# Attention's second head turned one place later, the query norms behind a weighing, and four sums of a down projection behind the next weights

## The chip, the cores and the metric

The kernel runs on one core of a Trainium2 chip. TensorE multiplies (PE in the profile; PEld is its weight load), VectorE and ScalarE (DVE, ACT) do the elementwise work, GpSimd (POOL) and SyncE (SP) mainly start transfers. The metric is the device time of one execution in microseconds (us); lower is better. Times are medians over runs.

## The reference

Two decoder layers over 512 tokens of width 1024, all in float32. Layer 0 is a Mamba-2 mixer with a convolutional feed-forward; then keys and values are made once; layer 1 is differential attention with eight heads, again with a feed-forward. What the change touches, cut to it:

```python
q = rms_norm((rms_norm(x, ln_g) @ q_w).reshape(b, s, 8, 2, 64), q_norm_g)   # query norms
logits = einsum(q, k) * 64 ** -0.5 + bias          # two maps per head, causal
p = softmax(logits)
attn = p[:, :, 0] - lam * p[:, :, 1]               # the "weighing"
o = rms_norm(einsum(attn, v), subln_g) * (1 - lam_init)   # a head's output
x = x + o @ out_w
u = causal_dwconv(rms_norm(x, ln_g) @ up_w)        # feed-forward of layer 1
x = x + (silu(u_gate) * u_up) @ down_w             # the "down" product
```

## The kernel before

Every float32 product is made of three products of rounded halves: a weight is split into `wh` (rounded, by ACT) and `wl` (the rest, by DVE: weight minus `wh`), and TensorE adds `wh*xh`, `wh*xl` and `wl*xh` in one PSUM bank (L207 to L209, L1325 to L1327, L1133 to L1136). `chunk(key)` takes the next weights of a fixed plan and starts the split of those two places ahead. There are eight PSUM banks: four for large products ("mm") and four for everything else ("aux": logits, transposes, values and some of the down products).

**Attention.** In this part the order on TensorE is written out by hand (`manual_schedule`); the orders of DVE and ACT are made by a list scheduler from the same program. A head is three units (`Unit`), named head_part: `lg3_0` is head 3, part 0. A unit goes through `logits` (TensorE into `lg` banks, DVE adds the bias and takes the maxima `mx`, ACT takes the exponentials with their sums `sm`), `weigh` (DVE: reciprocal `rc`, factor, then one sum per block of rows at L1525; part 0 has two of them, 128 and 256 wide), `turn` (TensorE transposes the weighed map into an `at` bank, L1534, ACT copies it out, L1535) and `values` (TensorE into `po`, L1545, ACT into `ot`). When a head's three units have their values, `normed_out` scales its output `ot` (ACT square, DVE sum `so`, two ACT steps, three small DVE steps and `ot` times `so` at L1558), and `turned_out` transposes it (`oT`, L1564) and splits it into `oh` (ACT) and `ol` (DVE) for the output product. `ots.append([t + 5, u])` sets at which place of the written order `turned_out` is issued.

Between the units TensorE works on what `fill` gives: the value projection `v0`, the queries of heads 4 to 7 (`q1`), the values `v1`, and the first output product. Each `next(fill)` is two blocks of 128 tokens against one chunk of weights (12 matmuls). The queries `q1` come out as four tiles `knq1_0` to `knq1_3`; `head_norm` multiplies them by their norms on DVE (L1350) and registers in `late` two transposes (`ktq1`, L1357) that TensorE does inside `v1`, and that ACT copies into `qT1`, which the logits of head 4 read.

**Down product of layer 1.** The feed-forward's 22 pairs of columns are done in three parts (0 to 5, 6 to 13, 14 to 21). After each part, `down_tokens` makes the down product with seven products instead of eight (keys 1, 2, 5, 7, 6, 3, 4, in this order). After product 6, DVE combines for b = 0 and 1: the running sum `run_sum` takes product 6, is subtracted from one stretch of the residual `xr`, takes product 7, and goes into two more stretches of `xr` (L1139). Product 3 is then added, product 4 last. `wl_s14_0_0` and `wl_s14_0_2` are the low halves of product 4's weights in the first part; `wl_g1_6` is that of the first gate weights of the next part. Here the scheduler orders all engines.

Of the kernel before, what the change touches and what calls it, by code (L numbers as in the profile page):

```python
# [18 lines left out]
P = 128  # L19
# [22 lines left out]
def trunk_kernel(ctx: ExitStack, tc, x, ssm_ln_g, ssm_in_w, ssm_conv_w, ssm_conv_b, ssm_dt_bias,  # L42
# [950 lines left out]
    def ffn(l, norm, bp, gnext, nnext):  # L993
        with tc.tile_pool(name="ffn_h%d" % l, bufs=1) as hp, tc.tile_pool(name="ffn%d" % l, bufs=1) as fp:
# [65 lines left out]
            def combine(key, m, p0, c, nq):  # L1060

                n = nq * ncol
                if m == "2" or (m == "4" and not l):
                    t = wrp.tile([P, 1024], F32, tag="raw", name="wr_" + key)
                    sync.dma_start(view(t, nq), source(p0, c, nq, 1, 0 if l or m == "2" else 1))
                elif l:
                    t = raws["x" if m == "7" else "y" if m == "3" else "z"][c // 2]
                    if m == "7":
                        dve.tensor_tensor(out=t[:, :n], in0=t[:, :n], in1=raws["y"][c // 2][:, :n], op=ALU.add)
                else:  # L1070
                    t = raws["x" if m in "17" else "z"][c]
                wh = wp.tile([P, 1024], F32R, tag="wh", name="wh_" + key)
                wl = wp.tile([P, 1024], F32R, tag="wl", name="wl_" + key)
                act.activation(wh[:, :n], t[:, :n], AF.Copy)
                dve.tensor_tensor(out=wl[:, :n], in0=t[:, :n], in1=wh[:, :n].bitcast(F32), op=ALU.subtract)  # L1075
                ready.append((key, view(wh, nq), view(wl, nq)))
                more = ({"1": (0, 1), "5": (1, 1), "6": (1, 0)} if l else {"1": (0, 1), "5": (0, 0), "6": (1, 0)}).get(m)
                if more:
                    plus(t, p0, c, nq, *more)
# [41 lines left out]
            def down_tokens(p0, n, sides, last):  # L1121

                nq = n // 2
                side = {"1": 0, "2": 1, "4": 2, "5": 3, "6": 4, "7": 5, "3": 6}

                def products(m, bs, qs, pss, first=True, end=True, cols=slice(0, 512)):

                    for low in range(2):
                        for b in bs:
                            for q in qs:  # L1130
                                h, w = (t[:, side[m], b * P:(b + 1) * P] for t in sides[q][:2])
                                if low:
                                    pe.matmul(pss[b], h, ws[q][1][:, cols], start=False, stop=end and q == qs[-1])  # L1133
                                    continue
                                pe.matmul(pss[b], h, ws[q][0][:, cols], start=first and q == qs[0], stop=False)  # L1135
                                pe.matmul(pss[b], w, ws[q][0][:, cols], start=False, stop=False)  # L1136

                def add(t, v, op=ALU.add):
                    dve.tensor_tensor(out=t, in0=t, in1=v, op=op)  # L1139

                def to(b, c, n=512):
                    return xr[:, b, c:c + n]

                def store(b, c, eng):
                    eng.dma_start(out[0, b * P:(b + 1) * P, c:c + 256], to(b, c, 256))

                def stores(bs, c):
                    for b in bs:
                        for j in range(2):
                            store(b, c + 256 * j, sync if j else act)  # L1150

                for m in SEVEN[1]:
                    pss = [(aux_bank if m in "273" else mm_bank)("ps_s%s_%d_%d" % (m, p0, b)) for b in range(2)]
                    cut = last and m == "4"
                    ws = {}
                    for q0 in range(0, nq, 2):
                        wh, wl = chunk("s1%s_%d_%d" % (m, p0, q0))
                        qs = range(q0, min(nq, q0 + 2))
                        for q in qs:
                            ws[q] = wh[:, q - q0, :], wl[:, q - q0, :]  # L1160
                        if not cut:
                            products(m, range(2), qs, pss, q0 == 0, qs[-1] == nq - 1)
                    if cut:
                        products(m, (0,), range(nq), pss)
                    for b in range(2):
                        r = run_sum[:, b, :]
                        if m == "1":
                            add(to(b, 0), pss[b])
                            act.activation(r, pss[b], AF.Copy)
                        elif m == "2":  # L1170
                            add(to(b, 0), pss[b])
                        elif m == "5":
                            add(to(b, 512), pss[b])
                            add(to(2 + b, 512), pss[b])
                        elif m == "7":
                            seven = pss
                        elif m == "6":
                            add(r, pss[b])
                            add(to(b, 512), r, ALU.subtract)
                            add(r, seven[b])  # L1180
                            add(to(2 + b, 512), r, ALU.subtract)
                            add(to(2 + b, 0), r)
                        elif m == "3":
                            add(to(b, 512), pss[b])
                        elif not (cut and b):
                            add(to(2 + b, 0), pss[b])
                    if last and m in "263":
                        stores((2, 3) if m == "6" else (0, 1), 0 if m == "2" else 512)
                    if cut:
                        stores((2,), 0)  # L1190
                        products(m, (1,), range(nq - 1), pss)
                        add(to(3, 0), pss[1])
                        for j in range(2):
                            end = aux_bank("end%d" % j)[:, :256]
                            products(m, (1,), [nq - 1], {1: end}, cols=slice(256 * j, 256 * (j + 1)))
                            add(to(3, 256 * j, 256), end)
                            store(3, 256 * j, act if j else sync)
# [85 lines left out]
    with tc.tile_pool(name="att", bufs=1) as ap, ExitStack() as later:  # L1283
# [61 lines left out]

        def head_norm(key, kn, ss, dst, gcol, where):
            rsqrt_act(ss, ap, key, [P, NT, 8], 64)
            for b in range(NT):
                v = kn[b].rearrange("p (a q) -> p a q", a=8)
                dve.tensor_tensor(out=v, in0=v, in1=ss[:, b, :].unsqueeze(2).to_broadcast([P, 8, 64]),  # L1350
                                  op=ALU.mult)

            def turned(bs):
                for b in bs:
# [263 lines left out]
        with tc.manual_schedule(engines={mybir.EngineType.PE}):  # L1618
# [17 lines left out]
            def values(t):  # L1636
                u = us[t]
                u.values()
                if u.part == len(PARTS) - 1:
                    valued_heads.append(u)  # L1640
                    ots.append([t + 5, u])

            def norm_heads():
                while valued_heads:
# [108 lines left out]
```

## Time and profile before

| | |
|---|---|
| median of 3 runs | 1323.74 us (1322.02 to 1325.03) |
| the profiled execution | 1323.59 us, of which the profile's span is 1321.9 us |
| TensorE busy | 1313.3 us, 99% of the span |
| VectorE busy | 1094.1 us, 83% |
| ScalarE busy | 722.5 us, 55% |
| mean granted TensorE clock | 0.999 |

The profile is of one execution. Its views have one row for a group of instructions: the engine, the source line, the operation, the tiles it writes and reads, how often it ran, and in brackets how long the engine had sat idle before it and what released it. In the timeline, the first number is the start from the beginning of the span, the second how long it took; neighbours of one kind are merged (x4). TensorE's instructions overlap: one begins before the last has drained, so its rate is read from the distances of the starts. Buffer numbers are left out in the timeline: `lg`, `at`, `oT`, `so` there are those of whichever head stands at that time.

### The profile page before, as it was taken

The page shows a single profiled execution, that of the slowest core. Times are in us where ns is not written, and L with a number is a line of the kernel's source. Part 1 is how long each engine was busy: PE and PEld are TensorE (multiplying, and loading weights), DVE is VectorE, ACT ScalarE, POOL GpSimd, SP SyncE. Part 2 cuts the span into 40 slices and gives each one's busy share as a digit, 9 for nine tenths or more (in the row PEclk, how much of TensorE's full clock was granted, in tenths as well). Part 3 has the DMA queues.
Part 4 walks back from the last instruction along what each step waited for, and adds up shares of the span by engine and source line. Part 5 has one row for each costly group of instructions (what it writes and reads, how often), then busy time and mean ns, then how long its engine had stood idle before and what let it go on. Part 6 is the DMA issues. An engine that isn't in the chain of part 4 may idle for free. (4 is left out here: it accounts for less than half of the span.)

```text
span 1321.9 us, 18303 instructions
## 1 busy us (share of the span) xinstructions
PE 1313.3 (99%) x6771; PEld 1097.8 (83%) x6771; DVE 1094.1 (83%) x1834; ACT 722.5 (55%) x1176; POOL 176.2 (13%) x243
## 2 busy tenths in 40 slices
PE   9999999999999999999999999999999999999998
PEld 8878888888888988898889887767888878888887
DVE  7989888788878878886889877778778978887887
ACT  6696554743454545543556676767654534444452
POOL 4330200300121401110113210000020100010001
PEclk9999999999999999999999999999999999999999
DMA  7553533532235657674856854211225445453635
GB/s 209 161 154 87 146 108 103 145 92 79 80 96 149 118 149 205 167 155 128 225 143 143 208 129 125 64 57 56 65 80 159 97 119 178 106 99 112 191 64 128
DMA packets 202553, 167.85 MB, mean 127 GB/s; under 512 B 7580, under 2 KB 175904, under 8 KB 202464
## 3 DMA queue, kind: packets, MB, share of 16 engines
q1 hardware_dynamic: 176080, 124.93, 31.8%
q0 software_dynamic: 22928, 36.46, 14.8%
q10 hardware_dynamic: 3456, 5.30, 1.1%
q8 instruction: 53, 0.87, 0.3%
q14 instruction: 36, 0.29, 0.1%
HBM read 160.21 MB, written 6.44 MB: 126 GB/s over the span
## 5 line engine op out<-in xcount | busy, mean ns | idle before, releaser
L207 PE MATMUL ps_u<-xgh,wh_u 128*128 128x512 f32 x352 | 137.4, 390 | 0.0
L209 PE MATMUL ps_g<-xgh,wl_g 128*128 128x512 f32 x352 | 137.1, 389 | 0.0
L207 PE MATMUL ps_g<-xgh,wh_g 128*128 128x512 f32 x352 | 137.1, 389 | 0.0
L209 PE MATMUL ps_u<-xgh,wl_u 128*128 128x512 f32 x352 | 137.0, 389 | 0.0
L208 PE MATMUL ps_g<-xgl,wh_g 128*128 128x512 f32 x352 | 137.0, 389 | 0.0
L208 PE MATMUL ps_u<-xgl,wh_u 128*128 128x512 f32 x352 | 136.9, 389 | 0.0
L207 PE MATMUL ps_in<-xgh,wh_in 128*128 128x512 f32 x304 | 122.9, 404 | 0.0
L209 PE MATMUL ps_in<-xgh,wl_in 128*128 128x512 f32 x304 | 119.7, 394 | 0.0
L208 PE MATMUL ps_in<-xgl,wh_in 128*128 128x512 f32 x304 | 119.1, 392 | 0.0
L209 PEld LDWEIGHTS ps_g<-xgh,wl_g 128*128 128x128 f32 x352 | 66.1, 188 | 14.0 <-DVE wl_g L158 0.3
L208 PEld LDWEIGHTS ps_g<-xgl,wh_g 128*128 128x128 f32 x352 | 66.1, 188 | 13.7
L1228 PE MATMUL ps_s<-sl,wh_s 128*128 128x256 f32 x308 | 77.5, 283 | 0.0
L209 PEld LDWEIGHTS ps_u<-xgh,wl_u 128*128 128x128 f32 x352 | 66.1, 188 | 13.7
L1227 PE MATMUL ps_s<-sh,wh_s 128*128 128x256 f32 x308 | 77.5, 283 | 0.0
L208 PEld LDWEIGHTS ps_u<-xgl,wh_u 128*128 128x128 f32 x352 | 66.1, 188 | 13.6
L207 PEld LDWEIGHTS ps_g<-xgh,wh_g 128*128 128x128 f32 x352 | 66.1, 188 | 13.6
L207 PEld LDWEIGHTS ps_u<-xgh,wh_u 128*128 128x128 f32 x352 | 66.1, 188 | 13.5
L1118 ACT ACTIVATE sh<-vg 128x256 fp32r<-128x256 f32 (+1 forms) x44 | 23.0, 524 | 96.0 <-DVE vg L1266 96.0
L1047 POOL DMA_DIRECT2D wz<-in_ffn_down_w_dram x36 | 44.2, 1295 | 233.3 <-DVE wl_s L1075 156.1
L1262 ACT ACTIVATE vg<-vg 128x512 f32<-128x512 f32 x44 | 27.8, 633 | 78.7 <-DVE vg L1019 78.7
L1019 DVE SCALAR_TENSOR_TENSOR vg<-ug,cf,vg 128x511 f32<-128x511 f32 x88 | 65.8, 748 | 5.5 <-ACT vg L1017 4.1
L147 ACT ACTIVATE wh_u<-wr_u 128x1024 fp32r<-128x1024 f32 x44 | 46.6, 1059 | 42.5 <-PE ps_g L208 35.4
(430 smaller groups left out, 3527.1 us busy)
## 6 DMA issues: line engine op xcount, KB each, us to landing
wr_g<-in_ffn_up_w_dram SPq DMA_DIRECT2D x44, 512.0 KB, 3.9
wr_u<-in_ffn_up_w_dram SPq DMA_DIRECT2D x44, 512.0 KB, 4.0
wr_in<-in_ssm_in_w_dram SPq DMA_DIRECT2D x40, 512.0 KB, 3.9
wz<-in_ffn_down_w_dram POOLq DMA_DIRECT2D x27, 512.0 KB, 5.9
m<-cumd POOLq DMA_DIRECT2D x16, 512.0 KB, 5.0
wr_out<-in_ssm_out_w_dram SPq DMA_DIRECT2D x16, 512.0 KB, 3.5
wr_s<-in_ffn_down_w_dram SPq DMA_DIRECT2D x13, 512.0 KB, 3.8
xT<-in_ffn_down_w_dram SPq DMA_DIRECT2D x10, 512.0 KB, 7.0
```

Of the source, the lines that this page charges most:

```text
L147: return act.activation(self.wh[:, :self.n], self.raw[:, :self.n], AF.Copy)
L207: pe.matmul(ps, wh, xh, start=start, stop=False)
L208: pe.matmul(ps, wh, xl, start=False, stop=False)
L209: return pe.matmul(ps, wl, xh, start=False, stop=stop).ins
L1019: dve.scalar_tensor_tensor(out=v[:, s:], in0=u[:, :T - s], scalar=col(2 - s), in1=v[:, s:], op0=ALU.mult, op1=ALU.add)
L1047: pool.dma_start(view(t, nq), source(p0, c, nq, j, i), accum_op=ALU.add)
L1118: act.activation(sh[:, o], v, AF.Copy)
L1227: pe.matmul(v[:, b], wh[:, q, cols], h, start=q == 0, stop=False)
L1228: pe.matmul(v[:, b], wh[:, q, cols], w, start=False, stop=False)
L1262: act.activation(ga, ga, AF.Silu)
```

## The change

Three edits. The output of head 1 is turned at `t + 6` instead of `t + 5`. The four multiplications of the `q1` norms are no longer issued when the queries are done, but registered in `late`, behind block 3 of the first `v1` chunk. In the first part of layer 1's down product (`p0 == 0`), the four sums of `run_sum` into the lower two blocks of `xr` are issued with product 3, behind the last low half that `combine` has made by then (`state["low"]`).

```diff
--- before.py
+++ after.py
@@ -1072,7 +1072,8 @@
                 wh = wp.tile([P, 1024], F32R, tag="wh", name="wh_" + key)
                 wl = wp.tile([P, 1024], F32R, tag="wl", name="wl_" + key)
                 act.activation(wh[:, :n], t[:, :n], AF.Copy)
-                dve.tensor_tensor(out=wl[:, :n], in0=t[:, :n], in1=wh[:, :n].bitcast(F32), op=ALU.subtract)
+                state["low"] = dve.tensor_tensor(out=wl[:, :n], in0=t[:, :n], in1=wh[:, :n].bitcast(F32),
+                                                 op=ALU.subtract).ins
                 ready.append((key, view(wh, nq), view(wl, nq)))
                 more = ({"1": (0, 1), "5": (1, 1), "6": (1, 0)} if l else {"1": (0, 1), "5": (0, 0), "6": (1, 0)}).get(m)
                 if more:
@@ -1143,6 +1144,11 @@
 
                 def store(b, c, eng):
                     eng.dma_start(out[0, b * P:(b + 1) * P, c:c + 256], to(b, c, 256))
+
+                def second_half(b):
+                    r = run_sum[:, b, :]
+                    add(to(2 + b, 512), r, ALU.subtract)
+                    add(to(2 + b, 0), r)
 
                 def stores(bs, c):
                     for b in bs:
@@ -1178,9 +1184,12 @@
                             add(r, pss[b])
                             add(to(b, 512), r, ALU.subtract)
                             add(r, seven[b])
-                            add(to(2 + b, 512), r, ALU.subtract)
-                            add(to(2 + b, 0), r)
+                            if p0:
+                                second_half(b)
                         elif m == "3":
+                            if not p0:
+                                with tc.issue_after(state["low"]):
+                                    second_half(b)
                             add(to(b, 512), pss[b])
                         elif not (cut and b):
                             add(to(2 + b, 0), pss[b])
@@ -1345,10 +1354,16 @@
 
         def head_norm(key, kn, ss, dst, gcol, where):
             rsqrt_act(ss, ap, key, [P, NT, 8], 64)
-            for b in range(NT):
-                v = kn[b].rearrange("p (a q) -> p a q", a=8)
-                dve.tensor_tensor(out=v, in0=v, in1=ss[:, b, :].unsqueeze(2).to_broadcast([P, 8, 64]),
-                                  op=ALU.mult)
+            def normed():
+                for b in range(NT):
+                    v = kn[b].rearrange("p (a q) -> p a q", a=8)
+                    dve.tensor_tensor(out=v, in0=v, in1=ss[:, b, :].unsqueeze(2).to_broadcast([P, 8, 64]),
+                                      op=ALU.mult)
+
+            if key == "q1":
+                late.append(((0, 3), normed))
+            else:
+                normed()
 
             def turned(bs):
                 for b in bs:
@@ -1638,7 +1653,7 @@
                 u.values()
                 if u.part == len(PARTS) - 1:
                     valued_heads.append(u)
-                    ots.append([t + 5, u])
+                    ots.append([t + (6 if u.h == 1 else 5), u])
 
             def norm_heads():
                 while valued_heads:
```

Line numbers in the changed kernel are up to 15 higher. What the edits do to the engines' orders stands in three places.

**Place 1: attention, around the turn of head 1's output.** TensorE, before: `po2_1` are the values of head 2's second unit, `oT1` the transposes of head 1's output, `ps_v1_2` a value product with the chunk `v1_0`.

```order
L1545 MATMUL po2_1_8281<-vt0_6961,at2_1_8180 128x128
L1545 MATMUL po2_1_8281<-vt1_6962,at2_1_8180 128x128
L1545 MATMUL po2_1_8281<-vt2_6963,at2_1_8180 128x128
L1564 MATMUL oT1_8286<-ident_77,ot1_8028 128x128 x4
L1325 MATMUL ps_v1_2_8234<-wh_v1_0_7964,xgh_86 128x512
L1326 MATMUL ps_v1_2_8234<-wl_v1_0_7965,xgh_86 128x512
L1327 MATMUL ps_v1_2_8234<-wh_v1_0_7964,xgl_87 128x512
```

TensorE in the changed kernel, where `oT1` now stands (one chunk later, `v1_2`, behind the transposes of the queries):

```order
L1336 MATMUL ps_v1_1_8229<-wh_v1_2_8088,xgl_87 128x512
L1372 MATMUL ktq1_2_8359<-ident_77,knq1_2_8157 128x128 x4
L1372 MATMUL ktq1_3_8365<-ident_77,knq1_3_8162 128x128 x4
L1579 MATMUL oT1_8371<-ident_77,ot1_8028 128x128 x4
L1334 MATMUL ps_v1_2_8230<-wh_v1_2_8088,xgh_86 128x512
L1335 MATMUL ps_v1_2_8230<-wl_v1_2_8089,xgh_86 128x512
L1336 MATMUL ps_v1_2_8230<-wh_v1_2_8088,xgl_87 128x512
```

The four transposes moved behind 24 matmuls of `v1`, one whole unit's turn, logits and values (`at3_0`, `lg3_2`, `po2_2`) and the four `ktq1` transposes.

VectorE at the same time, before: the first weighing of `lg3_0` (128 wide), the query norms, the second weighing (256 wide), the low half of head 1's output.

```order
L1525 SCALAR_TENSOR_TENSOR lg3_0_0_8192<-lg3_0_1_8193,sm3_0_8191,lg3_0_0_8192 128x128
L1350 TENSOR_TENSOR knq1_0_8106<-knq1_0_8106,ssq1_7751 128x512
L1350 TENSOR_TENSOR knq1_1_8111<-knq1_1_8111,ssq1_7751 128x512
L1350 TENSOR_TENSOR knq1_2_8157<-knq1_2_8157,ssq1_7751 128x512
L1350 TENSOR_TENSOR knq1_3_8162<-knq1_3_8162,ssq1_7751 128x512
L1525 SCALAR_TENSOR_TENSOR lg3_0_0_8192<-lg3_0_1_8193,sm3_0_8191,lg3_0_0_8192 128x256
L1568 SCALAR_TENSOR_TENSOR ol1_8292<-oT1_8286,c2_89,oh1_8291 128x512
```

VectorE in the changed kernel:

```order
L1540 SCALAR_TENSOR_TENSOR lg3_0_0_8192<-lg3_0_1_8193,sm3_0_8191,lg3_0_0_8192 128x128
L1540 SCALAR_TENSOR_TENSOR lg3_0_0_8192<-lg3_0_1_8193,sm3_0_8191,lg3_0_0_8192 128x256
L1360 TENSOR_TENSOR knq1_0_8106<-knq1_0_8106,ssq1_7751 128x512
L1360 TENSOR_TENSOR knq1_1_8111<-knq1_1_8111,ssq1_7751 128x512
L1360 TENSOR_TENSOR knq1_2_8157<-knq1_2_8157,ssq1_7751 128x512
L1360 TENSOR_TENSOR knq1_3_8162<-knq1_3_8162,ssq1_7751 128x512
L1519 ISA lg3_2_0_8306,mx3_2_8304<-lg3_2_0_8308,tb3_8186 128x512
```

The second weighing moved ahead of the four norms, and `ol1` went some rows further down, behind the weighing of `lg3_2`.

**Place 2: attention, some microseconds later.** ScalarE, before, from the exponentials of `lg3_2` on: the copies of the turned queries into `qT1`, the two steps of head 2's output norm `so2`, the high half of the first output weights.

```order
L1512 ACTIVATE lg3_2_1_8316,sm3_2_8314<-lg3_2_1_8316,mx3_2_8313 128x512
L1358 ACTIVATE qT1_6960<-ktq1_0_8350,c2_89 128x4x128
L1358 ACTIVATE qT1_6960<-ktq1_1_8356,c2_89 128x4x128
L495 ACTIVATE so2_8381<-rsm_o2_8384 128x4
L496 ACTIVATE so2_8381<-so2_8381 128x4
L1358 ACTIVATE qT1_6960<-ktq1_2_8368,c2_89 128x4x128
L1358 ACTIVATE qT1_6960<-ktq1_3_8374,c2_89 128x4x128
L147 ACTIVATE wh_ao0_0_8447<-wr_ao0_0_8445 128x1024
```

ScalarE in the changed kernel:

```order
L1527 ACTIVATE lg3_2_1_8307,sm3_2_8305<-lg3_2_1_8307,mx3_2_8304 128x512
L1373 ACTIVATE qT1_6960<-ktq1_0_8341,c2_89 128x4x128
L1373 ACTIVATE qT1_6960<-ktq1_1_8347,c2_89 128x4x128
L1373 ACTIVATE qT1_6960<-ktq1_2_8359,c2_89 128x4x128
L1373 ACTIVATE qT1_6960<-ktq1_3_8365,c2_89 128x4x128
L1582 ACTIVATE oh1_8376<-oT1_8371,c2_89 128x512
L495 ACTIVATE so2_8381<-rsm_o2_8384 128x4
L496 ACTIVATE so2_8381<-so2_8381 128x4
L147 ACTIVATE wh_ao0_0_8447<-wr_ao0_0_8445 128x1024
```

`oh1`, the high half of head 1's output, now stands behind all four copies, and the two steps of `so2` behind `oh1`. On VectorE the sum that makes `so2` stands behind `ol1`, which reads `oh1`.

**Place 3: the down product of layer 1's first part.** VectorE, before: `run_sum` takes product 7, goes into `xr` four times, then come the low halves of product 4, the sums of product 3, and the next part's gate weights.

```order
L1139 TENSOR_TENSOR run_sum1_9342<-run_sum1_9342,ps_s7_0_0_10026 128x512
L1139 TENSOR_TENSOR run_sum1_9342<-run_sum1_9342,ps_s7_0_1_10027 128x512
L1139 TENSOR_TENSOR xr_9339<-xr_9339,run_sum1_9342 128x512 x4
L1075 TENSOR_TENSOR wl_s14_0_0_10097<-wz1_0_9340,wh_s14_0_0_10096 128x1024
L1075 TENSOR_TENSOR wl_s14_0_2_10113<-wz1_1_9341,wh_s14_0_2_10112 128x512
L1139 TENSOR_TENSOR xr_9339<-xr_9339,ps_s3_0_0_10094 128x512
L1139 TENSOR_TENSOR xr_9339<-xr_9339,ps_s3_0_1_10095 128x512
L158 TENSOR_TENSOR wl_g1_6_10129<-wr_g1_6_10126,wh_g1_6_10128 128x1024
```

VectorE in the changed kernel:

```order
L1140 TENSOR_TENSOR run_sum1_9342<-run_sum1_9342,ps_s7_0_1_10027 128x512
L1075 TENSOR_TENSOR wl_s14_0_0_10093<-wz1_0_9340,wh_s14_0_0_10092 128x1024
L1075 TENSOR_TENSOR wl_s14_0_2_10109<-wz1_1_9341,wh_s14_0_2_10108 128x512
L1140 TENSOR_TENSOR xr_9339<-xr_9339,run_sum1_9342 128x512 x2
L1140 TENSOR_TENSOR xr_9339<-xr_9339,ps_s3_0_0_10090 128x512
L1140 TENSOR_TENSOR xr_9339<-xr_9339,run_sum1_9342 128x512 x2
L1140 TENSOR_TENSOR xr_9339<-xr_9339,ps_s3_0_1_10091 128x512
L158 TENSOR_TENSOR wl_g1_6_10129<-wr_g1_6_10126,wh_g1_6_10128 128x1024
```

The four sums moved behind the two low halves; `wl_g1_6` has the same instructions ahead of it as before. TensorE there, before (from the last products of the high half `wh_s14_0_0` on):

```order
L1135 MATMUL ps_s4_0_1_10125<-wh_s14_0_0_10096,sh2_9660 128x512
L1136 MATMUL ps_s4_0_1_10125<-wh_s14_0_0_10096,sl2_9661 128x512
L207 MATMUL ps_g1_6_10164<-xgh_86,wh_g1_6_10128 128x512
L208 MATMUL ps_g1_6_10164<-xgl_87,wh_g1_6_10128 128x512
L1133 MATMUL ps_s4_0_0_10124<-wl_s14_0_0_10097,sh0_9447 128x512
L1133 MATMUL ps_s4_0_0_10124<-wl_s14_0_0_10097,sh2_9660 128x512
L1133 MATMUL ps_s4_0_1_10125<-wl_s14_0_0_10097,sh0_9447 128x512
```

TensorE in the changed kernel, at the end of product 4:

```order
L1134 MATMUL ps_s4_0_0_10124<-wl_s14_0_2_10109,sh4_9837 128x512
L1134 MATMUL ps_s4_0_1_10125<-wl_s14_0_2_10109,sh4_9837 128x512
L207 MATMUL ps_g1_6_10164<-xgh_86,wh_g1_6_10128 128x512
L208 MATMUL ps_g1_6_10164<-xgl_87,wh_g1_6_10128 128x512
L207 MATMUL ps_u1_6_10202<-xgh_86,wh_u1_6_10146 128x512
L208 MATMUL ps_u1_6_10202<-xgl_87,wh_u1_6_10146 128x512
L209 MATMUL ps_g1_6_10164<-xgh_86,wl_g1_6_10129 128x512
```

The first two matmuls of the next gate product, which stood inside product 4 ahead of its low half, moved to its end. The first use of `wl_g1_6` follows, as before, behind product 4 and the first two matmuls of `u1_6`.

## Prediction

> **What bounds the kernel now.** I read the page first. TensorE is busy all through the span, so a change to the order can only win what TensorE stands still, and can only lose by making it stand still.
>
> ```profile
> PE 1313.3 (99%) x6771; PEld 1097.8 (83%) x6771; DVE 1094.1 (83%) x1834; ACT 722.5 (55%) x1176; POOL 176.2 (13%) x243
> ```
>
> The chain that ended last is TensorE throughout and tells no more, so I went to TensorE's own waits:
>
> ```profile
> PE oT L1564 <- DVE ot L1558: 2.8, 1, 2.8
> PE warm L291 <- DVE ones L218: 1.1, 1, 1.1
> PE ps_s L1133 <- DVE wl_s L1075: 0.7, 1, 0.7
> ```
>
> Three waits: the second is the start. The first is the turn of a head's output, waiting for its norm; the third is a down product waiting for a low half. The change touches both. The timeline says which head and what follows:
>
> ```profile
> 846.53 0.94 PE L1545 MATMUL po<-vt,at 128*128 128x128 f32 x6
> 847.30 0.60 PE L1564 MATMUL oT<-ident,ot 128*128 128x128 f32 x4
> 847.66 0.47 PE L1325 MATMUL ps_q<-wh_q,xgh 128*128 128x512 f32 x1
> ...
> 850.51 0.49 PE L1534 MATMUL at<-ident,lg 128*128 128x128 f32 x3
> ...
> 861.91 0.94 PE L1545 MATMUL po<-vt,at 128*128 128x128 f32 x6
> 865.61 1.03 PE L1564 MATMUL oT<-ident,ot 128*128 128x128 f32 x4 [2.76 <-DVE ot L1558]
> 866.30 0.78 PE L1325 MATMUL ps_v<-wh_v,xgh 128*128 128x512 f32 x1
> ...
> 870.46 0.49 PE L1534 MATMUL at<-ident,lg 128*128 128x128 f32 x3
> 870.88 1.13 PE L1498 MATMUL lg<-kT,qT 64*128 64x512 f32 x4
> ```
>
> The upper rows are the same stretch one head earlier, undisturbed: values to turn 0.77 us, the turn 0.36, twelve matmuls 2.85 (847.66 to 850.51). Head 1's turn starts at 865.61 instead of 862.68 (861.91 + 0.77), 2.93 us late; then the turn takes 0.69 and the twelve matmuls 4.16 (866.30 to 870.46), 1.64 us more than undisturbed. The stretches show why:
>
> ```profile
> 862.33:865.74 3.41, 0.65 (x6) 0.46 (x5) 2.60 (x17) 3.30 (x16) 0.00 (x0) 1.00 0.53 154
> 865.74:869.16 3.42, 3.42 (x11) 2.84 (x12) 3.42 (x9) 1.25 (x3) 0.00 (x0) 0.50 0.01 2
> ...
> 1064.00:1068.00 4.00, 3.28 (x15) 2.36 (x14) 4.00 (x6) 1.41 (x2) 0.00 (x0) 1.00 0.00 0
> ```
>
> In the first stretch TensorE was busy 0.65 of 3.41 us; in the second its granted clock (the figure after the five engines) was 0.50. The last row is the stretch of the third wait, with 0.72 us of rest: the clock stayed at 1.00. So head 1's turn costs 2.93 + 1.64 = 4.6 us, 0.35%. That, with the third wait, is all there is to win.
>
> **Edit 1 and 2: head 1's turn, query norms.** With `oT1` gone, TensorE goes at 862.68 from the values into the twelve matmuls of `v1` and reaches the turn `at3_0` 2.85 us later, at 865.5. That needs both weighings of `lg3_0` on VectorE:
>
> ```profile
> 864.87 0.68 DVE L1558 TENSOR_TENSOR ot<-ot,so 128x512 f32<-128x512 f32 x1
> 865.83 0.35 DVE L1525 SCALAR_TENSOR_TENSOR lg<-lg,sm,lg 128x128 f32<-128x128 f32 x1
> 866.10 2.49 DVE L1350 TENSOR_TENSOR knq<-knq,ssq 128x512 f32<-128x512 f32 x4
> 868.50 0.48 DVE L1525 SCALAR_TENSOR_TENSOR lg<-lg,sm,lg 128x256 f32<-128x256 f32 x1
> ```
>
> Up to 866.10 VectorE's and ScalarE's orders are unchanged and wait for nothing of TensorE's that moves. The second weighing takes the place of the norms: 866.10 + 0.48 = 866.58, and the handoff, as from `ot` (865.55) to `oT1` (865.61), 0.06: `at3_0` gets its second block at 866.64. Its first two transposes wait one by one, so the first is then done, and the logits of `lg3_2` start some 0.3 us later, at 866.95, where they started at 870.88: 3.93 us earlier. The turn itself is still to be paid behind the query transposes: 0.36. Gain: **3.57 us**. Without the second edit the second weighing would end 2.40 us later and the gain be 1.2: the norms behind it (to 868.9) are hidden, since their first reader `ktq1` stands 3.9 us behind `at3_0`, at 870.5. So a wait of about 1.1 us stays at `at3_0`. Bounds for it: none (VectorE just in time, +1.1) and the old 2.76 with its half clock; a wait of 1.1 is nearer to the 0.72 us of the third wait, where the clock stayed at 1.00, so I take it at its bare length.
>
> Behind it, `oT1` needs the bank that `ktq1_0` leaves. And the output norm of head 2 gets behind `oh1` and `ol1`. The rows of before, by which I follow that chain:
>
> ```profile
> 873.97 0.16 DVE L1507 TENSOR_SCALAR mx<-mx 128x2 f32<-128x2 f32 x1
> 874.70 0.68 DVE L1556 TENSOR_REDUCE so<-osq 128x4 f32<-128x512 f32 x1
> 877.20 0.16 DVE L497 TENSOR_TENSOR rst_o<-so 128x4 f32<-128x4 f32 x1 [0.27 <-ACT so L496]
> 877.79 0.69 DVE L1558 TENSOR_TENSOR ot<-ot,so 128x512 f32<-128x512 f32 x1
> 881.52 1.22 DVE L158 TENSOR_TENSOR wl_ao<-wr_ao,wh_ao 128x1024 fp32r<-128x1024 f32 x1 [3.04 <-ACT wh_ao L147]
> 882.67 0.28 DVE L1504 CUSTOM_DVE_ANT_0 lg<-lg,tb 128x128 f32<-128x128 f32 x1
> ...
> 874.17 0.72 ACT L1512 ACTIVATE lg<-lg,mx 128x512 f32<-128x512 f32 x1
> 875.60 1.24 ACT L1358 ACTIVATE qT<-ktq,c 128x512 f32<-128x512 f32 x2
> 876.74 0.20 ACT L495 ACTIVATE so<-rsm_o 128x4 f32<-128x4 f32 x1
> 884.10 0.40 ACT L1512 ACTIVATE lg<-lg,mx 128x128 f32<-128x128 f32 x1 [0.99 <-DVE mx L1507]
> 885.87 0.57 ACT L1535 ACTIVATE at<-at 128x512 f32<-128x512 f32 x1
> ...
> 887.19 0.60 PE L1564 MATMUL oT<-ident,ot 128*128 128x128 f32 x4
> ```
>
> In the changed kernel the norms end at 868.9; the two maxima of `lg3_2` with a piece of `wl_v` between them put `mx` at about 871.05. ScalarE: exponentials 0.20 behind it and 1.43 long (874.17 to 875.60), so the `qT1` copies run from 872.7, four of 0.57 each. The first is out by 873.3, just before TensorE wants its bank for `oT1` (873.5): no wait, with 0.2 to spare. `oh1` starts at 875.0, takes 0.69, `ol1` 0.66, the sum for `so` and its first step 0.7 more: 877.1. The two steps on ScalarE and back, 0.46 + 0.2; the small steps and `ot`, 0.6 + 0.6: VectorE is free at 878.9. Then `wl_ao`, which before began at 881.52 after 3 us of rest, that is at 878.0 on the shifted clock: VectorE is now **0.9 to 1.0 us late**. From its start to the exponentials of `lg4_0` are 2.58 us (884.10 - 881.52): 881.5; to the copy of `at3_2` on ScalarE 1.77 more; it ends at 883.85. TensorE's next turn, `oT2`, needs that copy's bank, and comes there at 887.19 - 3.57 = 883.6. Before, the copy was out 0.75 us ahead of it. So a new wait: **-0.25**, with bounds 0 and 1.0 (if the chain slips by as much again as it now lags). The weighing of `lg4_0` also falls behind another maximum (0.48 us), but is out at 885.6, 1.5 us before its turn.
>
> **Edit 3: the four sums.** The rows of this place:
>
> ```profile
> 1064.14 0.39 PE L207 MATMUL ps_g<-xgh,wh_g 128*128 128x512 f32 x1
> 1065.48 1.21 PE L1133 MATMUL ps_s<-wl_s,sh 128*128 128x512 f32 x4 [0.72 <-DVE wl_s L1075]
> 1068.42 0.50 PE L209 MATMUL ps_g<-xgh,wl_g 128*128 128x512 f32 x1
> ...
> 1060.61 1.28 DVE L1139 TENSOR_TENSOR run_sum<-run_sum,ps_s 128x512 f32<-128x512 f32 x2
> 1061.80 2.49 DVE L1139 TENSOR_TENSOR xr<-xr,run_sum 128x512 f32<-128x512 f32 x4
> 1064.21 1.82 DVE L1075 TENSOR_TENSOR wl_s<-wz,wh_s 128x1024 fp32r<-128x1024 f32 x2
> 1067.14 1.22 DVE L158 TENSOR_TENSOR wl_g<-wr_g,wh_g 128x1024 fp32r<-128x1024 f32 x1
> ...
> 1060.97 1.07 ACT L1074 ACTIVATE wh_s<-wz 128x1024 fp32r<-128x1024 f32 x1 [4.13 <-DMA wz<-in_ffn_down_w_dram]
> ```
>
> The low half of product 4 now comes at 1062.1 (ScalarE's `wh_s` ends at 1062.04, so VectorE waits 0.27 for it) and ends at 1063.3, before TensorE's 1064.14. The wait there, 0.9 us in start distances, goes. But VectorE works without a pause from 1060.61 to here, and the four sums still stand ahead of `wl_g1_6`. TensorE does its 14 matmuls (2 + 4 + 4 + 2 + 2) in 3.2 us and stands at the first use of `wl_g` at 1067.3. `wl_g` ends where it did (1068.36) plus the 0.27 that VectorE now waits: TensorE goes on at 1068.7 instead of 1068.42. The wait is moved five groups further, not removed: **-0.26**. Bounds: +0.9, if `wl_g` came in time, which the 2.41 us of sums still ahead of it exclude, and -0.5.
>
> **Sum.** 3.57 - 0.25 - 0.26 = 3.06 us less. The profiled execution took 1323.59 us, 0.15 under the median; from the median that is 1320.7. All three edits leave the queues of SP and POOL as they are.
>
> **A rule against it.** The row first: after 2.76 us of rest the clock was 0.50 for 3.42 us. The Trainium skill, TensorE: Matmul & The Clock Gate, Part 1: The HAM clock gate, says that the clock is halved after at least one idle window of about 3.4 us. The trace agrees with the length of the slow stretch and not with the rest needed, since 0.65 us of work in that window did not prevent it. By the rule taken strictly a rest of 2.76 us costs no half clock, and the sum would be 1.4.
>
> **Rivals.**
> - *The clock pays otherwise.* Nothing in the trace says that a rest of 2.76 us halves the clock each time; if in the timed runs of before it mostly did not, or if a rest of 1.1 us (`at3_0`) or 1.4 us (`wl_g`) halves it too, 1.64 us less is won: 3.06 - 1.64 = 1.4, 1322.3. For it: the three runs lie 3 us apart. Against: the profiled run, with the half clock, is at the median. 20%. The Trainium skill, TensorE: Matmul & The Clock Gate, Part 1: The HAM clock gate, gives one way to it: its windows run free, so that a rest may fall across two of them.
> - *Edit 3 removes its wait after all*, since `wl_g1_6` is not late or TensorE has slack there: 3.57 + 0.9, less 0.25 = 4.2: 1319.5. Against: VectorE's unbroken row of work. 15%.
> - *Slower.* The copies into `qT1` stand behind the exponentials of `lg3_2`; if these come late, `oT1` waits for its bank with everything behind it. A slip of 0.2 us is free, 3.3 takes the whole gain, 5.9 makes it 0.2% slower (1326.4). It would need a wait of several us on ScalarE or VectorE that no row here shows. 5%.
>
> **How the numbers follow.** My forecast has the other 60%, with 1319.9 to 1322 as its own range: the two small terms move by 0.7 together, the timed medians by about 1. A change under 0.2% (2.65 us) can't be told from none here; the line lies at 1321.1, close to my 1320.7. So of the 60%, 37 fall beyond it and 23 short of it; of the clock's 20, 3 and 17; of edit 3's 15, 14 and 1; of the last 5, 1 is short of it and 4 slower. Faster 0.54, same 0.42, slower 0.04. The range for 8 in 10 goes from edit 3's case less some scatter, 1318.9, to the clock's case plus some, 1323.3.
>
> **What would show it.** In the changed kernel's profile: no wait of `oT` for `ot`; a wait of about 1.1 us at the turn `at` (L1549 there) for VectorE's weighing, with the clock at 1.00 behind it; a short wait at a later `oT` for ScalarE; no wait at the low half of the down product, and 1.2 to 1.4 us at L209 for `wl_g` instead. Wrong would be: a clock of 0.50 after either rest, no wait at L209, or a wait at `ktq1` or at the logits of head 4.

## The result, and the profile after

The changed kernel took 1320.98 us (median of 12 runs, 1319.96 to 1321.74) against 1323.64 us before (12 runs): a ratio of 0.998, 95% interval 0.9972 to 0.9988. In a later job both ran side by side again: 1320.81 us (11 runs) against 1323.94 us (21 runs), ratio 0.9975, interval 0.9966 to 0.9984. The forecast was 1320.7 us.

First the engines' busy row of the changed kernel's page and TensorE's waits (total, count and longest in us):

```profile
PE 1311.2 (99%) x6771; PEld 1096.0 (83%) x6771; DVE 1095.6 (83%) x1834; ACT 722.7 (55%) x1176; POOL 176.8 (13%) x243
```

```profile
PE ps_g L209 <- DVE wl_g L158: 1.1, 1, 1.1
PE at L1549 <- DVE lg L1540: 0.6, 1, 0.6
PE ktq L1372 <- issue: 0.2, 1, 0.2
```

The wait of `oT` for `ot` (2.8 us) is gone and a shorter one at `at` has come; the wait at the low half of the down product (0.7 us) is gone and a longer one at L209 has come. (The wait at the start of the kernel, the same in both, is left out here.) The timeline shows what the first exchange gave, on TensorE and then on VectorE:

```profile
861.41 0.94 PE L1560 MATMUL po<-vt,at 128*128 128x128 f32 x6
...
864.71 0.39 PE L1336 MATMUL ps_v<-wh_v,xgl 128*128 128x512 f32 x1
865.72 0.83 PE L1549 MATMUL at<-ident,lg 128*128 128x128 f32 x3 [0.62 <-DVE lg L1540]
866.48 1.13 PE L1513 MATMUL lg<-kT,qT 64*128 64x512 f32 x4
...
873.05 0.60 PE L1579 MATMUL oT<-ident,ot 128*128 128x128 f32 x4
876.25 0.49 PE L1549 MATMUL at<-ident,lg 128*128 128x128 f32 x3
...
883.30 0.66 PE L1579 MATMUL oT<-ident,ot 128*128 128x128 f32 x4
886.56 0.49 PE L1549 MATMUL at<-ident,lg 128*128 128x128 f32 x3
```

```profile
864.36 0.68 DVE L1573 TENSOR_TENSOR ot<-ot,so 128x512 f32<-128x512 f32 x1
865.31 0.75 DVE L1540 SCALAR_TENSOR_TENSOR lg<-lg,sm,lg 128x128 f32<-128x128 f32 x2
865.97 2.49 DVE L1360 TENSOR_TENSOR knq<-knq,ssq 128x512 f32<-128x512 f32 x4
```

This execution was 0.50 us ahead already at the values that stand before the place of head 1's turn (`po` at 861.41, before 861.91). TensorE's instructions up to there are the same in both kernels, so this isn't the change's; I take it off everywhere. The logits of `lg3_2` then start 866.48 against 870.88: 4.40 - 0.50 = 3.90 us earlier. At `at3_1`, with the moved turn paid, 876.25 against 880.23 leaves 3.48. Further on, at `at4_0`, 886.56 against 890.40 leaves 3.34. The two rows of before for these are

```profile
880.23 0.49 PE L1534 MATMUL at<-ident,lg 128*128 128x128 f32 x3
...
890.40 0.49 PE L1534 MATMUL at<-ident,lg 128*128 128x128 f32 x3
```

VectorE's two weighings stand next to each other now and end at 866.06; TensorE, which started its last matmul of `v1` at 864.71 and would have gone on 0.23 us later, starts at 865.72.

The clock behind this rest is the figure behind the five busy times in this row, which is for one stretch:

```profile
865.72:869.13 3.41, 3.34 (x18) 2.14 (x19) 3.41 (x9) 2.15 (x5) 0.00 (x0) 1.00 0.00 0
```

It is 1.00 where the kernel before had 0.50. The place of the four sums, TensorE and then VectorE:

```profile
1060.30 1.07 PE L1134 MATMUL ps_s<-wl_s,sh 128*128 128x512 f32 x4
...
1064.78 0.50 PE L209 MATMUL ps_g<-xgh,wl_g 128*128 128x512 f32 x1 [1.15 <-DVE wl_g L158]
```

```profile
1058.16 1.83 DVE L1075 TENSOR_TENSOR wl_s<-wz,wh_s 128x1024 fp32r<-128x1024 f32 x2
1059.91 1.29 DVE L1140 TENSOR_TENSOR xr<-xr,run_sum 128x512 f32<-128x512 f32 x2
...
1063.51 1.22 DVE L158 TENSOR_TENSOR wl_g<-wr_g,wh_g 128x1024 fp32r<-128x1024 f32 x1
```

The low halves are early, TensorE begins with them at 1060.30 without a wait, and stands at the next product's `wl_g` instead, which VectorE begins behind the sums at 1063.51. From the first matmul of the place to that point TensorE has the same 14 matmuls in both kernels: 4.48 us (1064.78 - 1060.30) now, 4.28 (1068.42 - 1064.14) before. Edit 3 costs 0.20 us.

The same `po` also serves for the whole rest of the kernel. TensorE's last matmul, before and then in the changed kernel:

```profile
1317.88 0.28 PE L1133 MATMUL end<-wl_s,sh 128*128 128x256 f32 x1
...
1314.25 0.28 PE L1134 MATMUL end<-wl_s,sh 128*128 128x256 f32 x1
```

From `po` it is 455.97 us before (1317.88 - 861.91) and 452.84 in the changed kernel (1314.25 - 861.41): 3.13 us less. The changed kernel's second profile, of the later job, took 1321.51 us instead of 1319.96, but nearly all of that stands already at `po` (862.92); from there on it is 452.85. Two single profiles are therefore compared from a common instruction here, and not by their total times.

### The profile page after: what moved, and what is told of

Same layout as the page of the kernel before. It is cut to its first block, busy times and chain, and to the rows that moved or that the text cites. A ratio compares the mean times of both kernels' runs of the same rounds, so it can differ in the third digit from the quotient of the medians.

```text
span 1318.3 us, 18304 instructions
## 1 busy us (share of the span) xinstructions
PE 1311.2 (99%) x6771; PEld 1096.0 (83%) x6771; DVE 1095.6 (83%) x1834; ACT 722.7 (55%) x1176; POOL 176.8 (13%) x243
## 4 chain that ended last, share of the span: by engine, by line
PE 97%; DVE 2%; ACT 1%; issue 0%; DVEq 0%
PE ps_g L209 6%; PE ps_u L209 6%; PE ps_g L207 6%; PE ps_u L207 6%; PE ps_g L208 6%; PE ps_u L208 6%; PE ps_in L207 5%; PE ps_in L209 5%; PE ps_in L208 5%; PE ps_s L1234 3%; PE ps_s L1237 3%; PE ps_s L1236 3%; PE ps_s L1137 3%; PE ps_s L1136 3%; PE ps_s L1134 3%; PE ps_o L208 2%
## 5 line engine op out<-in xcount | busy, mean ns | idle before, releaser
L209 PE MATMUL ps_g<-xgh,wl_g 128*128 128x512 f32 x352 | 137.1, 389 | 1.1 <-DVE wl_g L158 1.1
L209 PE MATMUL ps_u<-xgh,wl_u 128*128 128x512 f32 x352 | 137.0, 389 | 0.0
L209 PE MATMUL ps_in<-xgh,wl_in 128*128 128x512 f32 x304 | 119.7, 394 | 0.0
L209 PEld LDWEIGHTS ps_g<-xgh,wl_g 128*128 128x128 f32 x352 | 66.0, 188 | 15.3 <-DVE wl_g L158 1.6
L209 PEld LDWEIGHTS ps_u<-xgh,wl_u 128*128 128x128 f32 x352 | 66.1, 188 | 13.7
```

The lines of the kernel that those rows point to most:

```text
L209: return pe.matmul(ps, wl, xh, start=False, stop=stop).ins
```

## Experiments

**Which edit carries it: four kernels with parts of the change.**

Edits 1 and 2 without edit 3:

```diff
+                late.append(((0, 3), normed))
...
+                    ots.append([t + (6 if u.h == 1 else 5), u])
```

> Edits 1 and 2 without edit 3. My theory: these two carry the whole gain, and edit 3 costs 0.2 to 0.3: 3.3 us less than before, about 1320.4 us, with the wait of 0.7 us at the low half of product 4 back and none at L209. Rival (edit 3 pays): 0.9 us more than the changed kernel, about 1321.8 us.

1320.71 us (11 runs, 1319.98 to 1321.55), ratio to before 0.9979 (0.997 to 0.9987); from `po` to the last matmul 452.63 us, 0.21 less than with edit 3. The two edits carry the whole gain. TensorE's waits in this kernel:

```profile
PE ps_s L1133 <- DVE wl_s L1075: 0.7, 1, 0.7
PE at L1540 <- DVE lg L1531: 0.6, 1, 0.6
```

The old wait at the low half is back, none at L209, and the time is not worse than with edit 3.

Edit 3 alone:

```diff
+                            if p0:
+                                second_half(b)
...
+                            if not p0:
+                                with tc.issue_after(state["low"]):
+                                    second_half(b)
```

> Edit 3 alone (the four sums behind the next product's first two pieces), head 1's turn and the norms as before. My theory: the wait at the low half of down product 4 (0.72 us) goes and a wait of 1.1 to 1.2 us at L209 for wl_g takes its place, so 0.2 to 0.3 us slower than before, about 1323.9 us; oT1 waits 2.7 to 2.9 us as before, with a clock of 0.50 behind it. Rival (edit 3 pays, its wait is removed): 0.9 us less, about 1322.7 us, and no wait at L209.

1324.42 us (11 runs) against 1324.14 of before in the same job, ratio 1.0005 (0.9997 to 1.0014): not told apart from no change; the rival's 0.9 us less (0.9993) lies outside the interval. The timeline says why:

```profile
1065.09 1.07 PE L1134 MATMUL ps_s<-wl_s,sh 128*128 128x512 f32 x4
...
1069.72 0.50 PE L209 MATMUL ps_g<-xgh,wl_g 128*128 128x512 f32 x1 [1.30 <-DVE wl_g L158]
```

4.63 us from the first row's start to the second's, 0.35 more than before.

Edit 1 alone, the turn moved and the norms left ahead of the weighing:

```diff
-                    ots.append([t + 5, u])
+                    ots.append([t + (6 if u.h == 1 else 5), u])
```

> Edit 1 alone: oT1 behind ktq1, the norms of q1 ahead of the second weighing of lg3_0 as before. My theory: at3_0's last two blocks get their weighing 2.4 us later than in the changed kernel, so TensorE stands some 3 us at at3_0. If such a rest halves the clock as the 2.76 us before oT1 did, the place is worth nothing, or 0.5 us less than nothing: 1323.5 to 1324.2 us. If it does not, 1.2 us less than before: 1322.5 us. Rival (edit 2 is not needed, the norms do not hold the weighing up): as fast as edits 1 and 2 together, 1320.4 us.

1324.98 us (11 runs, 1322.61 to 1325.61), ratio 1.0007 (0.9998 to 1.0015), 0.8 us above the range expected for a halved clock. No gain: without edit 2 the rest only moves from the turn to `at3_0`. The mean clock of each run tells more than the median: the fastest run, which is the profiled one, had 1.000, the ten others 0.997 or 0.999 and 1324.08 us or more. So the one run with an undisturbed clock came out as I had worked it out for that case (1322.5), and in the others the clock took more than the edit gave. A second profile of this kernel, below, shows it. TensorE's wait in the first:

```profile
PE at L1534 <- DVE lg L1525: 3.1, 2, 2.5
```

Edit 2 alone:

> Edit 2 alone: the norms of q1 behind the second weighing of lg3_0, oT1 ahead of v1's products as before. My theory: oT1 still waits 2.7 to 2.9 us for ot1, whose place on VectorE is the same, with the clock at 0.50 behind it; nothing is gained: 1323.6 us, within 0.3. Rival (the order of VectorE's work is what carries the gain): 1 to 3 us less.

1324.05 us (11 runs), ratio 1.0005 (0.9996 to 1.0014). TensorE's wait is the old one:

```profile
PE oT L1570 <- DVE ot L1564: 2.8, 1, 2.8
```

Edit 2 is worth nothing without edit 1, edit 1 nothing without edit 2.

**The halved clock by itself: the rest filled.** The kernel before, with transposes of the identity into the bank of `oT1` ahead of the four real ones, which overwrite them:

```diff
+            for _ in range(26 if h == 1 else 0):
+                pe.transpose(ps[:, :P], ident, ident)
             for i in range(NT):
                 pe.transpose(ps[:, i * P:(i + 1) * P], ot[:, i, :], ident)
```

> The kernel before with 26 transposes of the identity into oT1's bank ahead of the real four (2.3 us of TensorE work in the 2.8 us of rest); the result is the same. My theory: the rest before oT1 costs 2.9 us by itself and a halved clock behind it 1.6 us more in most runs; with the rest filled the clock stays at 1.00 in every run and the median falls by about 1.6 us, to the times that the kernel before shows in its runs with a clock of 1.000 (1321.8 to 1322.5). Rival (the halved clock is not what makes the slower runs): no change, 1323.7 to 1324.1 us.

1323.68 us (11 runs), ratio 1.0001 (0.9992 to 1.001). The clock was 1.000 in all 11 runs, as expected, and the time didn't fall. The rows say why this experiment gained nothing:

```profile
862.38 0.94 PE L1545 MATMUL po<-vt,at 128*128 128x128 f32 x6
864.61 3.06 PE L1564 MATMUL oT<-ident 128*128 128x128 f32 x26 [1.29 <-DVE mx L1504]
867.50 0.60 PE L1566 MATMUL oT<-ident,ot 128*128 128x128 f32 x4
```

The bank of `oT1` is read by VectorE's maxima until 1.5 us into the rest, so the 26 could only start then, and they held the real turn up: 867.50 - 862.38 = 5.12 us behind `po`, where before it was 3.70 (865.61 - 861.91). I had taken the cost of a halved clock (1.64 us) away on one side and put 1.42 us of my own on the other. The next turn, `at3_0`, starts 8.32 us behind `po` (870.70 - 862.38), before 8.55 (870.46 - 861.91): 0.23 less, which is what the two leave. With 9 transposes they are over in time:

> As the run with 26 transposes, with 9 of them (1.0 us by that run's 0.11 us each), so that they end before ot1 is ready and the real turn stands where it did before. My theory: TensorE's rest is 1.7 us and then 0.5 us, the clock stays at 1.00 behind it in all runs, and the median is that of the kernel before in its undisturbed-clock runs: about 1322.2 us. Rival: 1323.7 to 1324.1 us, as before.

1322.42 us (11 runs) against 1324.19, ratio 0.9987 (0.9978 to 0.9996). The real turn stands where it did, 3.68 us behind `po`:

```profile
862.02 0.94 PE L1545 MATMUL po<-vt,at 128*128 128x128 f32 x6
864.24 1.20 PE L1564 MATMUL oT<-ident 128*128 128x128 f32 x9 [1.28 <-DVE mx L1504]
865.70 0.66 PE L1566 MATMUL oT<-ident,ot 128*128 128x128 f32 x4 [0.26 <-DVE ot L1558]
...
868.96 0.61 PE L1534 MATMUL at<-ident,lg 128*128 128x128 f32 x3
```

`at3_0` stands 6.94 us behind `po` instead of 8.55: 1.61 us, with the real turn where it was. That is the halved clock alone in one execution (the prediction had 1.64); 1.38 of it are left at the last matmul. In the medians, nine matmuls that compute nothing make the kernel 1.77 us faster (1324.19 - 1322.42; by the interval 0.5 to 2.9). Edits 1 and 2 gave 3.43 in their job (1324.14 - 1320.71); the other 1.7 or so, by this difference, is the shorter rest itself.

**How much rest halves the clock.** With 3 transposes the rest is broken but not filled:

> The same with 3 transposes (0.33 us): rests of 1.7 us and 1.1 us with 0.33 us of work between. If the rest inside one window of 3.41 us is summed (threshold near 1.8 us, worked out from how many runs of before were halved), about half of the runs have a halved stretch and the median lies between 1322.2 and 1323.9 us. If only an unbroken rest counts, none has, and the median is 1322.2 us.

1324.17 us (11 runs), ratio 0.9996 (0.9987 to 1.0005). Nine of eleven runs took 1323.4 us or more, two 1321.61 and 1322.11. So a short piece of work in the rest doesn't save the clock, and rest inside a window is summed; but by their times more runs were hit than the half that I had worked out. And a second profile each of edit 1 alone and of the kernel before:

> Edit 1 alone, profiled once more. In the ten slower runs of eleven the mean clock was 0.997 or 0.999, in the profiled one 1.000. My theory: this profile shows one or two stretches of 3.41 us at a clock of 0.50 right behind the rest at at3_0, and 1324 to 1325.5 us; in the one run without, the rest of 0.64 and 2.48 us fell across an edge of the 3.41 us windows, 1.5 us into one and 1.65 us into the next. Rival (the slower runs have another cause): a clock of 1.00 at this place and 1324 us or more.

> The kernel before, profiled once more: 1321.8 to 1322.5 us if no window behind oT1's rest is halved, 1323.6 to 1324 us with one, 1324.3 to 1325 us with two. Rival (clock and time are not tied): any other pairing.

1325.79 us at a mean clock of 0.997, and 1324.24 us at 0.998. The second is 0.2 us above what was expected for one halved window, and has one; 0.72 us of its difference to the first profile stand already at `po` (862.63). The windows of the clock can be placed in each trace: in the clock's records the stretches at 0.50 behind such a rest begin 252 or 253 times 3.413 us after the first rise of the clock, and the same count gives the edges in an execution that has no such stretch. The rows by stretches, cut at those edges; each has the length, then the busy time of TensorE, of its weight load and of three other engines, and the clock. In this order: edit 1 alone in its first profile (two windows), the same in its second (three), 3 transposes (two), the second profile of before (two):

```profile
864.18:867.60 3.42, 1.85 (x8) 1.07 (x6) 3.42 (x17) 3.31 (x9) 0.00 (x0) 1.00 0.37 129
867.60:871.01 3.41, 1.87 (x10) 0.94 (x10) 3.34 (x8) 0.53 (x2) 0.00 (x0) 1.00 0.00 0
```

```profile
865.50:868.91 3.41, 0.79 (x4) 0.17 (x2) 3.41 (x10) 2.38 (x6) 0.00 (x0) 1.00 0.08 28
868.92:872.33 3.41, 2.94 (x7) 1.11 (x8) 2.14 (x7) 0.49 (x1) 0.00 (x0) 0.50 0.10 19
872.33:875.74 3.41, 3.41 (x13) 3.02 (x13) 2.12 (x7) 1.58 (x4) 0.00 (x0) 0.50 0.42 139
```

```profile
863.50:866.91 3.41, 1.19 (x9) 0.87 (x9) 2.71 (x16) 3.30 (x14) 0.00 (x0) 1.00 0.49 154
866.92:870.32 3.40, 3.40 (x10) 2.63 (x10) 3.40 (x8) 0.82 (x3) 0.00 (x0) 0.50 0.01 2
```

```profile
863.52:866.92 3.40, 0.65 (x6) 0.60 (x6) 2.75 (x16) 3.29 (x14) 0.00 (x0) 1.00 0.46 154
866.93:870.34 3.41, 3.41 (x10) 2.64 (x9) 3.41 (x7) 0.77 (x2) 0.00 (x0) 0.50 0.01 2
```

A window with 0.65, 0.79 or 1.19 us of TensorE's work was followed by one at half clock; windows with 1.85 and 1.87 us were not. The first two pairs are the same program with the same rest of 3.1 us: in one execution it fell across an edge and halved no clock, in the other most of it lay in one window, and TensorE needed 2.92 us more from `po` to its last matmul (457.81 against 454.89). There the clock stayed down for a second window too, behind one with 2.94 us of work; where the halved window was busy all through (the last two pairs), it was at 1.00 again in the stretch behind it. For that second window there is this one case.

**Where edit 3 should have put the sums.** The changed kernel with the sums two more low halves down, behind `wl_g1_6` and `wl_u1_6`:

```diff
             if self.gcol is None:
                 self.high()
-                self.low()
+                state["low"] = self.low().ins
...
                         elif m == "3":
+                            add(to(b, 512), pss[b])
+                        elif not (cut and b):
                             if not p0:
                                 with tc.issue_after(state["low"]):
                                     second_half(b)
-                            add(to(b, 512), pss[b])
-                        elif not (cut and b):
                             add(to(2 + b, 0), pss[b])
```

> The changed kernel with the four sums moved on by two more low halves, behind wl_g1_6 and wl_u1_6. My theory (edit 3 fails because the sums still stand ahead of wl_g1_6): wl_g is then out by 1062.3 us on the changed kernel's time, before TensorE asks for it, both waits of this place are gone, and 1.2 to 1.4 us less than the changed kernel: about 1319.7 us. Rival (TensorE is then held by the sums' banks or the next low half, so the wait moves on once more): within 0.3 us of the changed kernel.

1319.64 us (5 runs, 1318.92 to 1319.75) against the changed kernel's 1320.81 (11 runs, 1320.13 to 1322.32) in the same job, 1.17 less; ratio to before 0.9965 (0.9952 to 0.9979). From `po` to the last matmul it is 451.35 us, 1.49 less than in the changed kernel. TensorE and VectorE:

```profile
1063.22 0.39 PE L207 MATMUL ps_g<-xgh,wh_g 128*128 128x512 f32 x1
1063.44 0.39 PE L208 MATMUL ps_g<-xgl,wh_g 128*128 128x512 f32 x1
1063.67 0.39 PE L209 MATMUL ps_g<-xgh,wl_g 128*128 128x512 f32 x1
...
1061.82 1.22 DVE L158 TENSOR_TENSOR wl_g<-wr_g,wh_g 128x1024 fp32r<-128x1024 f32 x1
```

`wl_g` is begun at 1061.82 and out 0.6 us before TensorE reads it; both waits of the place are gone, and no other has come.

**The rest at `at3_0`.** On top of that, the scaling of `ot1` put behind both weighings and the norms:

```diff
-                late.append(((0, 3), normed))
+                late.append(((0, 3), lambda: (normed(), scaled_out.pop(0)())))
...
-            dve.tensor_tensor(out=ot, in0=ot, in1=so.unsqueeze(2).to_broadcast([P, NT, P]), op=ALU.mult)
+            def scaled():
+                with tc.issue_after(us[9].weighed) if h == 1 else nullcontext():
+                    dve.tensor_tensor(out=ot, in0=ot, in1=so.unsqueeze(2).to_broadcast([P, NT, P]), op=ALU.mult)
...
+            if h == 1:
+                scaled_out.append(scaled)
...
```

> The kernel with the sums behind both gate and up low halves, and besides ot1's scaling behind both weighings of lg3_0 and the query norms. My theory: both weighings come 0.6 us earlier, so the 0.7 to 0.8 us that TensorE still loses at at3_0 falls to 0.1 to 0.2 us, while ot1 is out 3.3 us later than before and oT1 still has it in time: 0.6 us less than the kernel with only the sums moved, about 1319.1 us. Rival (oT1 waits for the later ot1, or knq for ktq1): no gain or up to 1 us more.

1318.89 us (5 runs, 1318.7 to 1320.08), 0.75 less in the median; but the ranges of the five and five runs overlap, and so do the intervals of the ratios to before (here 0.9962, 0.995 to 0.9975). TensorE, with one row of ScalarE:

```profile
863.02 0.94 PE L1561 MATMUL po<-vt,at 128*128 128x128 f32 x6
867.49 1.13 PE L1514 MATMUL lg<-kT,qT 64*128 64x512 f32 x4
...
874.42 0.66 PE L1587 MATMUL oT<-ident,ot 128*128 128x128 f32 x4 [0.20 <-ACT qT L1374]
...
884.30 0.57 ACT L1551 ACTIVATE at<-at 128x512 f32<-128x512 f32 x1
...
884.92 0.66 PE L1587 MATMUL oT<-ident,ot 128*128 128x128 f32 x4
```

From `po` to the logits of `lg3_2` it is 4.47 us, in the changed kernel 5.07 (866.48 - 861.41): the 0.6 us that was expected there. But `oT1` now waits 0.20 us, not for `ot1` but for a bank that ScalarE's copies into `qT1` leave, the spot where the prediction had found 0.2 us to spare; and by `oT2` the whole gain is lost: 21.90 us behind `po` (884.92 - 863.02) against 21.89 in the changed kernel (883.30 - 861.41). `oT2` starts 0.05 us behind the end of ScalarE's copy (884.30 + 0.57), and that copy begins where it did, 21.28 us behind `po` against 21.27. By these rows it is that copy, whose bank `oT2` needs, that sets the time there, and what TensorE had won ahead of it is lost in waiting for it. To the last matmul it is 451.36 us, as without the move (451.35): the profiles show no gain, and the 0.75 us of the medians can't be put down to the move. The profiled execution, the slowest of its five, was 0.98 us behind already at `po` (863.02 against 862.04 without the move).

The changed kernel itself in that job:

> The changed kernel, for a comparison in the same job: 1321.0 us, clock 1.000 in all runs; 0.2 to 0.3 us over edits 1 and 2 alone (1320.7 us).

1320.81 us, 0.1 above edits 1 and 2 alone in the other job, where 0.2 to 0.3 were expected; the mean clock was 1.000 in ten runs and 0.999 in one. That one (1321.51 us) is the profiled one, and its only halved stretch is the end of the span, where TensorE has no work left:

```profile
1318.10:1319.80 1.70, 0.00 (x0) 0.00 (x0) 0.00 (x0) 0.00 (x0) 0.00 (x0) 0.50 0.09 30
```

So a mean of 0.999 or 0.998 alone does not tell how many windows were halved under load.

## Why the prediction was right

- **Edits 1 and 2, 3.57 us.** Measured 3.48 at `at3_1` in the trace. The new wait was sized right: the logits were to come 3.93 us earlier and came 3.90. The list of waits puts down only 0.62 us, where the prediction had said 1.1: the profile counts idle time from the modelled end of the last matmul, while the starts stand 1.01 us apart instead of 0.23, and the wait for the second weighing adds 0.34 (turn to logits 0.76, before 0.42). That without the second edit the gain would be only 1.2 was still too good: edit 1 alone had 1.1 of it in its one undisturbed run (from `po` on 454.89 us against 455.97) and none in the median, since its rest halves the clock too. Of the things that would have made it wrong none came: the 0.2 us at `ktq` in the list of waits has no releaser but issue, and stands in the second profile of before as well.
- **The halved clock, 1.64 us of those 3.57.** Shown by filling the rest: 1.61 us at `at3_0` in the trace, 1.77 of the median. The rival that it pays otherwise had its point: of 75 later runs of the kernel before, 7 had a mean clock of 1.000 (median 1322.29 us) and 14 one of 0.997 (median 1324.79 us); that is two halved windows, worked out from 2 x 3.41 us at half clock in 1322. Of the others 37 had 0.999 (median 1323.76 us) and 16 had 0.998 (1324.16); one shows 0.949 at an ordinary time, which stays unexplained. So it was in part luck that the profiled execution, with one halved window, was about as slow as the median. That the rest that stays (a wait of 1.1) does not halve the clock held in all 12 runs of the result.
- **The rule set against it.** By the Trainium skill, TensorE: Matmul & The Clock Gate, Part 1: The HAM clock gate, taken strictly, the windows run free, and it takes an idle one to halve the clock. The runs agree with the first half (the same rest was followed by a halved clock in one execution and not in another) and not with the second: 1.19 us of work in a window did not prevent it.
- **The new wait at `oT2`, 0.25 us.** The turn starts 0.88 us behind `po` (883.30 - 882.42), undisturbed 0.77: 0.11, and by `at4_0` 0.14 of the gain is lost. The chain came as it was followed. VectorE and ScalarE in the changed kernel:

```profile
878.34 1.22 DVE L158 TENSOR_TENSOR wl_ao<-wr_ao,wh_ao 128x1024 fp32r<-128x1024 f32 x1
...
882.68 0.57 ACT L1550 ACTIVATE at<-at 128x512 f32<-128x512 f32 x1
```

With the 0.50 added, `wl_ao` begins at 878.84 (worked out: 878.9) and the copy ends at 883.75 (883.85). TensorE came 0.1 us later than worked out, and so half of the small wait was not there. The profile puts it down to no engine; but the turn starts 0.05 us behind the copy's end (883.25 and 883.30), and where TensorE came earlier (the kernel with the scaling moved) `oT2` stayed at the copy's end.
- **Edit 3, 0.26 us lost.** Measured 0.20 in the changed kernel, 0.35 alone, and +0.28 us in the medians of edit 3 alone, where the interval includes no change. "The wait is moved five groups further, not removed" is what the rows show, and moving the sums behind `wl_g1_6` removes it.
- **The sum, 3.06 us.** The trace has 3.48 - 0.14 - 0.20 = 3.14, and 3.13 from `po` to the last matmul. The medians differ by 2.66 and 3.13 us in the two jobs; that the forecast of 1320.7 lies within 0.3 us of both medians of the changed kernel is in part luck, since the medians of the kernel before alone lie between 1323.64 and 1324.19 in the four jobs.

## What to carry to other kernels

A list of waits tells where an engine rests, but a wait is removed only if the work that was late is no longer behind something that is not needed yet: edit 3 moved four sums behind two pieces of work and left them ahead of the third, and the wait went there, a little longer. Two moves may be worth nothing each and 3 us together, when the first takes the engine to the next thing that is late; follow the order to the next late producer before you count the gain. Compare two profiles from an instruction that both share: in the last move (the scaling of `ot1`) medians of five runs said 0.75 us, and the traces from `po` on said that nothing was won, because another engine's copy held TensorE a little later. And where TensorE must rest some 2 us, the price is not only the rest: look at the clock of the stretch behind it, and at the mean clock of every run.

## What the runs showed of the hardware

In the traces of this case, TensorE's clock was halved for 3.41 us after a window of 3.41 us in which TensorE worked 1.19 us or less (busy time as the profile models it), and not after windows with 1.85 us; I had reckoned with an unbroken rest of nearly 3 us. Whether a rest of 3 us is hit depends on where the windows fall in that execution: one program took 454.89 us from `po` on in one execution and 457.81 in another. And the clock can stay down for a second window when the halved one has rest in it (2.94 us of work in 3.41; one case). Where between 1.19 and 1.85 us the limit lies was not tried, and no kept trace has a window between them.
